# Where the last head's sample projection and the far key scores stand in one step of a hybrid decoder

## The chip, the cores and the metric

The kernel runs on one core of one Trainium2 chip. The metric is the device time of one launch in microseconds. A core has TensorE (PE), VectorE (DVE), ScalarE (ACT), GpSimd (POOL), and SyncE (SP), which here only issues DMAs. Each engine works through its own instructions in order; semaphores tie the engines together.

## The reference

One layer, for a prompt of 512 tokens and for 8 sample sequences of 4 new tokens each, which share all weights. Of the mixer, what matters here is the attention of the sample tokens to a cache of 512 keys, at three dilations:

```python
z_q, z_k, z_v, z_conv, z_mq, z_gate = split_combined(h @ lw['w_in'])
q, k, v = attention_qkv(z_q, z_k, z_v, pos, lw)           # per-head RMSNorm and partial rotary
k_all = jnp.concatenate([cache_k, k], axis=1)             # 8 x (512 + 4) x 4 heads x 128
for g, (window, dilation) in enumerate(((128,1), (512,4), (2048,16))):
    o, l = dilated_gather_attention(q[:, :, 4*g:4*g+4], k_all, v_all, window, dilation)
a = combine_dilated(outs, lses) @ lw['w_attn_proj']
c = conformer_tail(conv of glu(z_conv)); m = memory attention(z_mq) @ lw['w_mem_proj']
x1 = x + (sigmoid(g_a)*a + sigmoid(g_c)*c + sigmoid(g_m)*m) @ w_out
y  = x1 + hier_moe(rms_norm(x1))                          # 32 experts, 6 MB of weights each
state: k_win_sample = k_all[:, 4:], v_win_sample = v_all[:, 4:], ...
```

## The kernel before

**Stages.** The program first normalises and transposes the inputs, then takes four heads in turn, then the conformer input (the "glu" products), the attention of the sample tokens, three gated output branches, `w_out` and the routing, and at last 32 experts whose 201 MB of weights stream in from HBM.

**A head.** `project_head(h, units)` multiplies the transposed tokens with three 128x8x256 weight units (queries of two dilations; queries of the third and keys; values and memory queries). Each unit is split into a high and a low part, the high by ACT and the low by DVE (`split`, line 231), and each product takes three matmuls (lines 237 to 239). `norm_vecs` (line 377) then norms the heads: squares on ACT, the root on POOL, the scaling on DVE. `attend_head(h)` computes the prompt's attention of a head: scores into PSUM, exponentials, transposes, copies of them by DVE (`PT`, lines 507 and 541), products with the values. The list scheduler lets the attention of head h run among the products of head h+1. The PSUM pool `mm`, through which all products go, has three buffers, so a product waits until the norms of the one three before it have been read out.

**The sample part of a head.** `sample()` inside `project_head` computes the 32 sample tokens' heads from the unsplit units (48 matmuls, line 404). It writes two queries per head to DRAM scratch, `q1d` and `q2d`, by DMAs that POOL issues (lines 415 and 416).

**Far scores.** Dilations 4 and 16 over the cache are done on DVE and not as matmuls. `far_scores(b)`, for each of the 8 sequences, loads 1 MB of cached keys and 1 MB of the queries, which are broadcast from `q1d` to all 128 partitions, multiplies them (line 591) and sums (line 592). `wide_scores(a)` does the same twice for the other dilation from `q2d` (lines 601 and 602). All of them are written ahead of the last head's attention (`h == 3`). `q1d` holds all four heads, so the first broadcast load waits for the sample part of the last head.

**Buffers and the load queue.** Units, cached keys, broadcasts and values all lie in `ring`, six buffers of 1 MB. SP issues nearly all loads, in one order that the scheduler fixes. A load whose buffer is still read holds up every load behind it.

**After the heads.** `glu(c)` multiplies conformer unit c with the tokens (lines 694 to 696). Three units follow the heads; the fourth (`c3`) is multiplied in the sample section. There `mem_scores(bp)` and `weighted(...)` compute the scores against the cached memory keys and the weighted sums of cached values (line 918). Then `branch_loads` fetches and splits the first weights of the output branches, and `branch` starts. The 16 new cache rows (`k_win_sample`, `v_win_sample`) are written by POOL (lines 688 and 690).

Of the kernel before, what the change touches and what calls it, by code (L numbers as in the profile page):

```python
# [11 lines left out]
F32 = mybir.dt.float32  # L12
# [5 lines left out]
ALU = mybir.AluOpType  # L18
# [3 lines left out]
P = 128  # L22
# [4 lines left out]
DB = 8  # L27
# [125 lines left out]
def build(tc, I, O, cols):  # L153
# [44 lines left out]
    def nm(s):  # L198
        cnt[0] += 1
        return f"{s}_{cnt[0]}"  # L200
# [4 lines left out]
    def v8(t):  # L205
        return t.rearrange("p (k c) -> p k c", k=8)
# [159 lines left out]

    def norm_vecs(ps, A, vecs, gains, rows):
        n = len(vecs)
        ms = hs_.tile([P, 4], F32, name=nm("hms"), tag="hms", bufs=4)
        sq = hs_.tile([P, HD], BF16, name=nm("sq"), tag="sq")  # L370
        for q, (pv, av) in enumerate(vecs):
            nc.scalar.activation(sq[:rows], ps[pv], AF.Square, scale=SC, accum_out=ms[:rows, q:q + 1])
        r = hs_.tile([P, 4], F32, name=nm("hrs"), tag="hrs", bufs=4)
        nc.gpsimd.tensor_scalar(r[:rows, :n], ms[:rows, :n], EPS, None, op0=ALU.add)
        nc.gpsimd.tensor_tensor(r[:rows, :n], r[:rows, :n], nhalf[:rows].to_broadcast([rows, n]), op=ALU.pow)
        for q, (pv, av) in enumerate(vecs):
            nc.vector.scalar_tensor_tensor(A[av], ps[pv], r[:rows, q:q + 1], gains[q],
                                           op0=ALU.mult, op1=ALU.mult)
# [17 lines left out]
    def project_head(h, units):  # L396
# [3 lines left out]
        def sample():  # L400
            psS = mm.tile([P, 512], F32, name=nm("mm"), tag="mm")
            for k in range(8):
                for j, u in enumerate((2, 0, 1)):
                    nc.tensor.matmul(psS[32 * j:32 * j + 32, :256], hTs[:, k, :], v8(units[u])[:, k, :],
                                     start=(k == 0), stop=(k == 7))
            sA = hs_.tile([P, 2, HD], F32, name=nm("sA"), tag="sA", bufs=1)
            s3 = psS[:96, :256].rearrange("p (c d) -> p c d", c=2)
            idx = [(slice(0, 96), c, slice(0, HD)) for c in range(2)]
            norm_vecs(s3, sA, [(x, x) for x in idx], [gsm[:96, 0], gsm[:96, 1]], 96)
            nc.scalar.copy(vS[:32, h, :], psS[:32, 0:HD])  # L410
            sc_, ss_ = rope_t[:96, 2 * P:2 * P + 32], rope_t[:96, 2 * P + 32:CF0 - P]
            rope(sA[:96].unsqueeze(1), sc_.unsqueeze(1).unsqueeze(1).to_broadcast([96, 1, 2, 32]),
                 ss_.unsqueeze(1).unsqueeze(1).to_broadcast([96, 1, 2, 32]), [96, 1, 2])
            nc.gpsimd.tensor_copy(kS[64:96, h, :], sA[64:96, 1, :])
            nc.gpsimd.dma_start(q1d[:, :, h, :].rearrange("b t d -> (b t) d"), sA[32:64, 1, :])
            nc.gpsimd.dma_start(q2d[:, :, h, :].rearrange("b t d -> (b t) d"), sA[64:96, 0, :])
            psT = tr.tile([P, 512], F32, name=nm("tr"), tag="tr")
            for c in range(2):
                nc.tensor.transpose(psT[:, c * 96:(c + 1) * 96], sA[:96, c, :], ident[:96, :96])
            nc.vector.tensor_copy(Ts[:, h].rearrange("p a q -> p (a q)"), psT[:, :192])  # L420
# [50 lines left out]
    def attend_head(h, T, vh, vp):  # L471
# [48 lines left out]
        for ip in range(2):  # L520
# [20 lines left out]
            nc.vector.tensor_copy(PT, pt.rearrange("p a b t -> p (a b) t"))  # L541
# [43 lines left out]
    marks = []  # L585

    def far_scores(b):
# [3 lines left out]
        nc.vector.tensor_tensor(qb, kb, qb, op=ALU.mult)  # L591
# [3 lines left out]
    def wide_scores(a):  # L595
# [5 lines left out]
        nc.vector.tensor_tensor(qb, kb, qb, op=ALU.mult)  # L601
# [31 lines left out]
    TV = project_head(0, w0)  # L633
    for h in range(4):
        nxt = [load_cols(w_in, c) for c in cols_h(h + 1)] if h < 3 else None
        if h == 3:
            def cload(c, t=None):
                return load_cols(w_in, [(CCOL + c * P, P), (CCOL + 512 + c * P, P)], t)

            cu = []  # L640
            for c in range(NGH):
                far_scores(2 * c)
                far_scores(2 * c + 1)
                cu.append(cload(c))
            far_scores(6)
            far_scores(7)
            for a in range(2):
                wide_scores(a)
# [110 lines left out]

    for c in range(NGH):  # L760
        glu(c, cu[c], st_tile)
        glus[0] += 1
# [5 lines left out]
    trs = tr  # L768

# [160 lines left out]
    for bp in range(2):  # L930
        mem_scores(bp)
    far_rows()
# [7 lines left out]
    for bp in range(2, 4):  # L940
        mem_scores(bp)
# [8 lines left out]
    glu(3, c3, kt_tile, ring)  # L950
    glus[0] += 1
# [734 lines left out]
```

## Time and profile before

| | us |
|---|---|
| median of 3 runs | 1192.67 (1192.16 to 1195.36) |
| the profiled execution | 1193.17 |
| its span, first to last instruction | 1191.4 |
| PE busy | 1112.9 (93%) |
| DVE busy | 526.5 (44%) |
| ACT, POOL busy | 294.9, 291.4 |
| DMA read and written | 324 MB, 272 GB/s |

A share of the whole span says little here, since the stages have different limits. The rows below therefore go by stretches of the span. A busy PE counts overlapping matmuls once, and a PE at the lower clock is busy as well.

### The profile page before, as it was taken

The numbers are of one execution on the slowest core, as the hardware profiler recorded it, in microseconds if no ns is written. First come the engines' busy times: TensorE is split into PE (matmuls) and PEld (weight loads), VectorE is DVE, ScalarE is ACT, GpSimd is POOL, SyncE is SP. The second block draws the span as 40 slices with busy tenths as digits, with TensorE's granted clock in tenths as the row PEclk, the third lists the DMA queues.
The fourth block names the chain that finished last, engine by engine and source line by source line (L and its number), as shares of the span: only waits on it lengthen the run. The fifth ranks groups of instructions, "written<-read, shape, count | busy, mean of one in ns | idle before, by whom it ended". The sixth has DMA issues, their size and how long they took to land. (4 is left out here: it accounts for less than half of the span.)

```text
span 1191.4 us, 21761 instructions
## 1 busy us (share of the span) xinstructions
PE 1112.9 (93%) x8964; PEld 827.6 (69%) x8965; DVE 526.5 (44%) x974; ACT 294.9 (25%) x723; POOL 291.4 (24%) x465
## 2 busy tenths in 40 slices
PE   6999999989289999999999998999999999999986
PEld 5998888988174899999998853555555555555442
DVE  6634444596385799947433255112224211122111
ACT  7433443432032432244322223000000000000000
POOL 5453434560048520212223010111111111111111
PEclk9999999999699999999999998999999999999998
DMA  9952210497867998313309377999999999999995
GB/s 323 230 156 76 62 38 28 170 369 218 217 254 257 365 381 311 106 36 107 142 6 353 128 301 292 413 409 411 415 413 410 412 412 408 407 391 405 405 408 228
DMA packets 116036, 323.85 MB, mean 272 GB/s; under 512 B 15273, under 2 KB 72177, under 8 KB 88032
## 3 DMA queue, kind: packets, MB, share of 16 engines
q1 hardware_dynamic: 105520, 310.10, 69.2%
q0 software_dynamic: 7664, 10.70, 3.8%
q10 hardware_dynamic: 2752, 1.65, 0.5%
q8 instruction: 71, 1.16, 0.4%
q14 instruction: 29, 0.24, 0.1%
HBM read 310.18 MB, written 31.49 MB: 287 GB/s over the span
## 5 line engine op out<-in xcount | busy, mean ns | idle before, releaser
L694 PE MATMUL mm<-hTh,hi 128*128 128x272 f32 x512 | 150.8, 295 | 7.5 <-DVE u L745 6.4
L1540 POOL DMA_INDIRECT out_y_all<-work,ids x32 | 49.9, 1558 | 437.5 <-DVE work L1539 399.7
L696 PE MATMUL mm<-hTh,lo 128*128 128x272 f32 x512 | 149.7, 294 | 0.0
L695 PE MATMUL mm<-hTl,hi 128*128 128x272 f32 x512 | 149.4, 292 | 0.0
L1536 PE MATMUL pd<-w,work 128*64 128x512 f32 x512 | 119.3, 608 | 0.6 <-issue 0.6
L1516 PE MATMUL pu<-w,xgT 128*64 128x256 f32 x992 | 113.5, 380 | 4.6 <-DMA w<-in_w_expert_up 3.5
L1516 PE MATMUL pg<-w,xgT 128*64 128x256 f32 x992 | 112.9, 380 | 1.2 <-DVE xgT L1336 0.9
L237 PE MATMUL mm<-hi,hTh 128*128 128x256 f32 x384 | 110.3, 287 | 0.0
L239 PE MATMUL mm<-hi,hTl 128*128 128x256 f32 x384 | 110.1, 287 | 0.0
L238 PE MATMUL mm<-lo,hTh 128*128 128x256 f32 x384 | 110.0, 286 | 0.0
L1516 PEld LDWEIGHTS pg<-w,xgT 128*64 128x64 f32 x992 | 71.0, 137 | 49.8 <-issue 16.2
L1526 DVE TENSOR_TENSOR work<-work,pu 128x256 f32<-128x256 f32 x32 | 19.5, 608 | 194.5 <-PE pu L1516 194.5
L694 PEld LDWEIGHTS mm<-hTh,hi 128*128 128x128 f32 x512 | 98.2, 192 | 10.3 <-DVE u L745 6.9
L1516 PEld LDWEIGHTS pu<-w,xgT 128*64 128x64 f32 x992 | 70.5, 137 | 43.0 <-DMA w<-in_w_expert_up 6.6
L695 PEld LDWEIGHTS mm<-hTl,hi 128*128 128x128 f32 x512 | 98.3, 192 | 0.5 <-issue 0.4
L696 PEld LDWEIGHTS mm<-hTh,lo 128*128 128x128 f32 x512 | 97.9, 192 | 0.4 <-issue 0.4
L231 DVE TENSOR_TENSOR lo<-w,hi 128x2048 fp32r<-128x2048 f32 (+2 forms) x46 | 82.1, 1802 | 35.9 <-ACT hi L230 35.9
L715 DVE SCALAR_TENSOR_TENSOR cT<-u,cT 128x512 f32<-128x512 f32 x120 | 88.9, 763 | 1.3
L1536 PEld LDWEIGHTS pd<-w,work 128*64 128x64 f32 x512 | 34.6, 139 | 62.8 <-issue 59.8
L1330 PE MATMUL px<-h,ohs 64*64 64x512 f16 (+1 forms) x558 | 72.4, 388 | 4.8 <-DVE gates L1412 2.9
L1026 POOL TENSOR_TENSOR z<-z,gth 128x272 f32<-128x272 f32 x32 | 35.6, 1116 | 163.9 <-DVE gth L1025 163.9
L237 PEld LDWEIGHTS mm<-hi,hTh 128*128 128x128 f32 x384 | 72.5, 189 | 2.3 <-issue 2.2
(459 smaller groups left out, 2058.8 us busy)
## 6 DMA issues: line engine op xcount, KB each, us to landing
w<-in_w_expert_gate SPq DMA_DIRECT2D x64, 1024.0 KB, 10.5
w<-in_w_expert_up SPq DMA_DIRECT2D x64, 1024.0 KB, 10.4
w<-in_w_expert_down SPq DMA_DIRECT2D x64, 1024.0 KB, 10.5
w<-in_w_in SPq DMA_DIRECT2D x30, 512.0 KB, 7.0
w<-in_w_in SPq DMA_DIRECT2D x12, 1024.0 KB, 13.0
w<-in_cache_k SPq DMA_DIRECT2D x10, 1024.0 KB, 11.4
w<-q1d SPq DMA_DIRECT2D x8, 1024.0 KB, 11.3
out_k_win_sample<-in_cache_k SPq DMA_DIRECT2D x8, 1016.0 KB, 14.5
```

The lines of the kernel that those rows point to most:

```text
L231: last_lo[0] = e.tensor_tensor(lo[:, s], v8(t)[:, s], hi[:, s].bitcast(F32), op=ALU.subtract)
L237: nc.tensor.matmul(ps, xh[k], wh[k], start=(k == 0), stop=False)
L238: nc.tensor.matmul(ps, xh[k], wl[k], start=False, stop=False)
L239: nc.tensor.matmul(ps, xl[k], wh[k], start=False, stop=(k == n - 1))
L694: nc.tensor.matmul(ps, wh[k], xh[k], start=(k == 0), stop=False)
L695: nc.tensor.matmul(ps, wh[k], xl[k], start=False, stop=False)
L696: nc.tensor.matmul(ps, wl[k], xh[k], start=False, stop=(k == n - 1))
L715: nc.vector.scalar_tensor_tensor(cTf[:, c, :NP], u[:, c, j:j + NP], w, cTf[:, c, :NP], op0=ALU.mult, op1=ALU.add)
L1330: nc.tensor.matmul(px[CAP * f:CAP * f + CAP], oh[:64 if i == 4 else P, i, :], src[:, 4 * f:4 * f + 4, :], start=(i == GORD[0] and r == 0), ...
L1516: last = nc.tensor.matmul(ps[CAP * f:CAP * f + CAP], xT[:, k, :], ws[k // 4][:, k % 4, 256 * f:256 * f + 256], start=(k == 0), stop=(k == 7))
L1536: last = nc.tensor.matmul(pd[CAP * f:CAP * f + CAP], hT[:, kk % 2, CAP * (kk // 2):CAP * (kk // 2) + CAP], w[4 + kk // 2][:, kk % 2, 512 * ...
L1540: nc.gpsimd.indirect_dma_start(out=y2, out_offset=bass.IndirectOffsetOnAxis(ap=idc2, axis=0), in_=o, in_offset=None, bounds_check=2 * NT - ...
```

## The change

- `sample` becomes a function of its own. For the last head it is called inside the projection of the third head (index 2), at its second unit and with high priority. To have the weights there, the units of heads 2 and 3 are loaded together, after head 0.
- `q1d` and `q2d` are written by SP and not by POOL.
- The far scores of sequences 0 to 2 are written ahead of the third head's attention, those of 3 to 7 ahead of the last head's. Each product is done in two halves of 1024 columns, and is held behind the last norm of the third head's projection (`far_pin`).
- The two wide scores come after the heads, and their products are held behind the last copy of attention probabilities (`last_att`).
- The fourth conformer unit is multiplied before the weighted sums, right after all memory scores, and the values of sequences 4 and 5 are loaded after it.
- The new cache rows are written by SP, after the load of that unit.

```diff
-    def project_head(h, units):
+    def sample(h, units):
 ...
-            nc.gpsimd.dma_start(q1d[:, :, h, :].rearrange("b t d -> (b t) d"), sA[32:64, 1, :])
-            nc.gpsimd.dma_start(q2d[:, :, h, :].rearrange("b t d -> (b t) d"), sA[64:96, 0, :])
+        nc.sync.dma_start(q1d[:, :, h, :].rearrange("b t d -> (b t) d"), sA[32:64, 1, :])
+        nc.sync.dma_start(q2d[:, :, h, :].rearrange("b t d -> (b t) d"), sA[64:96, 0, :])
 ...
+    def project_head(h, units, nxt=None):
 ...
                 if u * 2 + ip == (SPOS if h == 0 else 0):
-                    sample()
+                    if h < 3:
+                        sample(h, units)
+                if nxt is not None and (u, ip) == (1, 0):
+                    with tc.high_priority():
+                        sample(h + 1, nxt)
 ...
-        nc.vector.tensor_tensor(qb, kb, qb, op=ALU.mult)
+        for f in range(2):
+            fs = slice(1024 * f, 1024 * f + 1024)
+            with tc.issue_after(far_pin[0].ins):
+                nc.vector.tensor_tensor(qb[:, fs], kb[:, fs], qb[:, fs], op=ALU.mult)
 ...
-        nc.vector.tensor_tensor(qb, kb, qb, op=ALU.mult)
+        with tc.issue_after(last_att[0].ins):
+            nc.vector.tensor_tensor(qb, kb, qb, op=ALU.mult)
 ...
     for h in range(4):
-        nxt = [load_cols(w_in, c) for c in cols_h(h + 1)] if h < 3 else None
+        for g in {0: (1,), 1: (2, 3)}.get(h, ()):
+            U[g] = [load_cols(w_in, c) for c in cols_h(g)]
+        if h == 2:
+            far_pin.append(last_norm[0])
+            for b in range(3):
+                far_scores(b)
 ...
             for c in range(NGH):
-                far_scores(2 * c)
-                far_scores(2 * c + 1)
                 cu.append(cload(c))
+                far_scores(3 + c)
             far_scores(6)
             far_scores(7)
-            for a in range(2):
-                wide_scores(a)
 ...
-            TV = project_head(h + 1, nxt)
-    for b in range(DB):
-        nc.gpsimd.dma_start(O["k_win_sample"][0, b, PAST - DT:], kS[64 + DT * b:64 + DT * b + DT])
-    for b in range(DB):
-        nc.gpsimd.dma_start(O["v_win_sample"][0, b, PAST - DT:], vS[0 + DT * b:0 + DT * b + DT])
+            TV = project_head(h + 1, U[h + 1], U[3] if h == 1 else None)
 ...
+    for a in range(2):
+        wide_scores(a)
     for c in range(NGH):
         glu(c, cu[c], st_tile)
 ...
-    vs = [v_load(b) for b in range(4)]
-    vs += [v_load(4, "hi"), v_load(5, "lo")]
     mks += [pair_load(mk_src, 2), pair_load(mk_src, 3)]
     c3 = cload(3, wslot("hi"))
+    new_rows()
+    vs = [v_load(b) for b in range(4)]
 ...
-    for bp in range(2):
+    for bp in range(4):
         mem_scores(bp)
+    glu(3, c3, kt_tile, ring)
+    glus[0] += 1
+    vs += [v_load(4, "hi"), v_load(5, "lo")]
     far_rows()
```

Of DVE's order before, the end of the last head's projection: `w` are ring buffers (keys and queries of the far scores), `lo` is a low part of a unit, `A` the normed heads of the product that the PSUM buffer of the first glu product held before.

```order
L591 TENSOR_TENSOR w_3260<-w_3259,w_3260 128x2048
L541 COPY PT_2716<-tr_2711 128x512
L592 TENSOR_REDUCE S_100<-w_3260 128x4x4
L591 TENSOR_TENSOR w_3266<-w_3265,w_3266 128x2048
L541 COPY PT_2740<-tr_2735 128x512
L592 TENSOR_REDUCE S_100<-w_3266 128x4x4
L420 COPY Ts<-tr_2797 128x192
L231 TENSOR_TENSOR lo_3684<-w_3271,hi_3683 128x2048
L377 SCALAR_TENSOR_TENSOR A_3080<-mm_3031,hrs_3087,gq 128x128
L377 SCALAR_TENSOR_TENSOR A_3080<-mm_3031,hrs_3087,gk 128x128
```

The same place on DVE after the change, ending at the norms of the same product.

```order
L600 TENSOR_TENSOR w_3296<-w_3295,w_3296 128x1024 x2
L535 TENSOR_SCALAR m_2794<-m_2794 128x2
L541 TENSOR_SCALAR P_2772<-P_2772,den_2771 128x256 x2
L601 TENSOR_REDUCE S_100<-w_3296 128x4x4
L513 COPY PT_2753<-tr_2749 128x256
L539 RECIPROCAL den_2795<-den_2795 128x2
L600 TENSOR_TENSOR w_3303<-w_3302,w_3303 128x1024 x2
L541 TENSOR_SCALAR P_2796<-P_2796,den_2795 128x256 x2
L601 TENSOR_REDUCE S_100<-w_3303 128x4x4
L547 COPY PT_2785<-tr_2780 128x512
L547 COPY PT_2809<-tr_2804 128x512
L379 SCALAR_TENSOR_TENSOR A_3101<-mm_3052,hrs_3108,gq 128x128
```

Before, four far scores stand ahead of these norms and four behind them; now all eight stand ahead, and the last of them directly so.

DVE before, in the last head's attention: the two wide scores (`S_101`) among the copies `PT` that PE waits for.

```order
L507 COPY PT_3384<-tr_3381 128x128
L601 TENSOR_TENSOR w_3302<-w_3301,w_3302 128x2048
L499 TENSOR_TENSOR P_3435<-P_3435 128x96
L500 RECIPROCAL m_3434<-m_3434 128x1
L745 SCALAR_TENSOR_TENSOR u<-st_3737,mm_3687 128x272
L602 TENSOR_REDUCE S_101<-w_3302 128x4x4
L601 TENSOR_TENSOR w_3314<-w_3313,w_3314 128x2048
L528 TENSOR_REDUCE m_3511<-S_3508 128x2
L507 COPY PT_3420<-tr_3416 128x256
```

DVE after, at the end of the last head's attention.

```order
L547 COPY PT_3510<-tr_3505 128x512
L759 SCALAR_TENSOR_TENSOR u<-st_3893,mm_3843 128x240
L761 SCALAR_TENSOR_TENSOR us<-st_3893,mm_3843 128x8x4
L547 COPY PT_3534<-tr_3529 128x512
L611 TENSOR_TENSOR w_3541<-w_3540,w_3541 128x2048
L611 TENSOR_TENSOR w_3553<-w_3552,w_3553 128x2048
L612 TENSOR_REDUCE S_101<-w_3541 128x4x4
L612 TENSOR_REDUCE S_101<-w_3553 128x4x4
```

No attention copy stands behind a wide score any more; all four wide instructions follow the last copy.

SP before, at the end of the sample section: values, memory values, and the first weights of the branches.

```order
L846 DMA w_4374<-in_cache_v 128x2048
L846 DMA w_4376<-in_cache_v 128x2048
L852 DMA w_4420<-in_cache_mem_v 128x2x512 x2
L852 DMA w_4423<-in_cache_mem_v 128x2x512 x2
L852 DMA w_4426<-in_cache_mem_v 128x2x512 x2
L852 DMA ws_4417<-in_cache_mem_v 128x2x512 x2
L218 DMA w_4600<-in_w_in 128x8x256
```

SP after, the same place.

```order
L863 DMA w_4507<-in_cache_v 128x2048
L869 DMA ws_4550<-in_cache_mem_v 128x2x512 x2
L863 DMA w_4509<-in_cache_v 128x2048
L869 DMA w_4553<-in_cache_mem_v 128x2x512 x2
L869 DMA w_4556<-in_cache_mem_v 128x2x512 x2
L869 DMA w_4559<-in_cache_mem_v 128x2x512 x2
L218 DMA w_4608<-in_w_in 128x8x256
```

The loads are nearly the same, but `w_4553`, `w_4556`, `w_4559` and `w_4608` now lie in the ring buffers of the values of sequences 0 to 3, which the first weighted sum reads to its end; and the fourth conformer unit's matmuls stand ahead of that sum on PE.

## Rows read from the trace of the kernel before

**Rows 1.** Busy time by stretches of the span; header line says the columns.
```profile
core 0: us, PE busy (x) PEld busy (x) DVE busy (x) ACT busy (x) POOL busy (x), PEclk, DMA share, GB/s
205.20:260.00 54.80, 51.69 (x448) 46.48 (x442) 38.99 (x64) 23.90 (x85) 32.14 (x53) 1.00 0.68 242
260.00:297.90 37.90, 36.21 (x310) 31.80 (x310) 27.82 (x42) 7.98 (x19) 6.62 (x16) 1.00 0.81 245
297.90:325.70 27.80, 4.22 (x17) 3.90 (x17) 8.40 (x9) 0.08 (x1) 0.00 (x0) 0.62 0.87 210
325.70:350.80 25.10, 21.53 (x180) 19.68 (x181) 22.87 (x42) 5.94 (x20) 8.22 (x19) 0.88 0.71 272
350.80:401.20 50.40, 48.81 (x446) 30.57 (x444) 29.59 (x63) 17.47 (x34) 43.22 (x99) 1.00 0.81 285
401.20:680.00 278.80, 278.80 (x2237) 269.77 (x2239) 170.01 (x265) 95.04 (x173) 57.77 (x87) 1.00 0.52 187
740.00:1160.00 420.00, 404.72 (x3085) 212.28 (x3085) 93.67 (x191) 28.47 (x59) 46.75 (x30) 1.00 1.02 409
```
**Rows 2.** PE in order of time: start us, us, instruction, [idle before <- releaser].
```profile
260.04 0.39 PE L694 MATMUL mm<-hTh,hi 128*128 128x272 f32 x1 [0.96 <-DVE A L377]
...
303.64 0.59 PE L694 MATMUL mm<-hTh,hi 128*128 128x272 f32 x1 [5.75 <-DVE u L745]
...
325.73 0.56 PE L511 MATMUL tr<-vh,PT 128*128 128x128 f32 x1 [17.87 <-DVE PT L507]
...
346.90 1.10 PE L544 MATMUL tr<-PT,mv 128*128 128x256 f32 x4 [2.24 <-DVE PT L541]
...
349.73 1.10 PE L544 MATMUL tr<-PT,mv 128*128 128x256 f32 x4 [1.29 <-DVE PT L541]
...
401.11 0.39 PE L694 MATMUL mm<-hTh,hi 128*128 128x272 f32 x1
```
**Rows 3.** DVE in order of time.
```profile
204.64 0.61 DVE L377 SCALAR_TENSOR_TENSOR A<-mm,hrs,gmq 128x128 f32<-128x128 f32 x2 [0.26 <-POOL hrs L375]
...
228.37 2.40 DVE L591 TENSOR_TENSOR w<-w,w 128x2048 f32<-128x2048 f32 x1 [0.97 <-DMA w<-q1d]
...
300.72 2.29 DVE L601 TENSOR_TENSOR w<-w,w 128x2048 f32<-128x2048 f32 x1 [9.50 <-DMA w<-q2d]
...
322.36 2.29 DVE L601 TENSOR_TENSOR w<-w,w 128x2048 f32<-128x2048 f32 x1 [16.58 <-DMA w<-in_cache_v]
```
**Rows 4.** Waits of the load queue: us in total, times, longest.
```profile
SPq L590 <- DMA q1d<-sA: 73.5, 1, 73.5
```
**Rows 5.** Busy time, as in rows 1, of two stretches at the lower clock.
```profile
303.60:307.90 4.30, 4.22 (x17) 3.90 (x17) 2.19 (x1) 0.00 (x0) 0.00 (x0) 0.50 1.07 200
...
325.70:331.80 6.10, 6.07 (x31) 5.49 (x32) 6.07 (x13) 0.94 (x3) 0.00 (x0) 0.50 0.98 370
```
**Rows 6.** Groups of instructions: xcount | busy us, mean ns | idle before.
```profile
L404 PE MATMUL mm<-w,hTs 128*32 128x256 f32 x192 | 16.8, 383 | 0.0
...
L591 DVE TENSOR_TENSOR w<-w,w 128x2048 f32<-128x2048 f32 x8 | 18.4, 2305 | 1.6 <-DMA w<-q1d 1.5
L592 DVE TENSOR_REDUCE S<-w 128x16 f32<-128x2048 f32 x8 | 18.3, 2282 | 0.1
...
L231 DVE TENSOR_TENSOR lo<-w,hi 128x1024 fp32r<-128x1024 f32 x6 | 7.2, 1222 | 5.2 <-ACT hi L230 5.2
```
**Rows 7.** DMA issues: xcount, KB each, median us from issue to landing.
```profile
w<-q1d SPq DMA_DIRECT2D x8, 1024.0 KB, 11.3
...
w<-q1d SPq DMA_DIRECT2D x1, 1024.0 KB, 4.3
...
w<-in_w_in SPq DMA_DIRECT2D x1, 1024.0 KB, 10.0
```
**Rows 8.** SP and ACT in order of time, end of the sample section.
```profile
371.83 4.45 SPq L852 DMA_DIRECT2D w<-in_cache_mem_v  x6
...
383.64 0.42 SPq L218 DMA_DIRECT2D w<-in_w_in  x1
...
394.04 1.90 ACT L230 CAST hi<-w 128x2048 fp32r<-128x2048 f32 x1
```

More of the change, by code (lines that the diff above doesn't have):

```diff
@@ L365, in cols_h @@
                 ((VCOL + h * P, P), (MQCOL + h * P, P)))
+    last_norm, far_pin = [None], []
     def norm_vecs(ps, A, vecs, gains, rows):
@@ L376, in norm_vecs @@
         for q, (pv, av) in enumerate(vecs):
-            nc.vector.scalar_tensor_tensor(A[av], ps[pv], r[:rows, q:q + 1], gains[q],
-                                           op0=ALU.mult, op1=ALU.mult)
+            last_norm[0] = nc.vector.scalar_tensor_tensor(A[av], ps[pv], r[:rows, q:q + 1], gains[q],
+                                                          op0=ALU.mult, op1=ALU.mult)
     def rope(A4, c4, s4, shape):
@@ L394, in bc4 @@
         return w.unsqueeze(2).to_broadcast([P, 2, 2, 32])
-    def project_head(h, units):
+    def sample(h, units):
+        psS = mm.tile([P, 512], F32, name=nm("mm"), tag="mm")
+        for k in range(8):
+            for j, u in enumerate((2, 0, 1)):
+                nc.tensor.matmul(psS[32 * j:32 * j + 32, :256], hTs[:, k, :], v8(units[u])[:, k, :],
+                                 start=(k == 0), stop=(k == 7))
+        sA = hs_.tile([P, 2, HD], F32, name=nm("sA"), tag="sA", bufs=2)
+        s3 = psS[:96, :256].rearrange("p (c d) -> p c d", c=2)
+        idx = [(slice(0, 96), c, slice(0, HD)) for c in range(2)]
+        norm_vecs(s3, sA, [(x, x) for x in idx], [gsm[:96, 0], gsm[:96, 1]], 96)
+        nc.scalar.copy(vS[:32, h, :], psS[:32, 0:HD])
+        sc_, ss_ = rope_t[:96, 2 * P:2 * P + 32], rope_t[:96, 2 * P + 32:CF0 - P]
+        rope(sA[:96].unsqueeze(1), sc_.unsqueeze(1).unsqueeze(1).to_broadcast([96, 1, 2, 32]),
+             ss_.unsqueeze(1).unsqueeze(1).to_broadcast([96, 1, 2, 32]), [96, 1, 2])
+        nc.gpsimd.tensor_copy(kS[64:96, h, :], sA[64:96, 1, :])
+        nc.sync.dma_start(q1d[:, :, h, :].rearrange("b t d -> (b t) d"), sA[32:64, 1, :])
+        nc.sync.dma_start(q2d[:, :, h, :].rearrange("b t d -> (b t) d"), sA[64:96, 0, :])
+        psT = tr.tile([P, 512], F32, name=nm("tr"), tag="tr")
+        for c in range(2):
+            nc.tensor.transpose(psT[:, c * 96:(c + 1) * 96], sA[:96, c, :], ident[:96, :96])
+        nc.vector.tensor_copy(Ts[:, h].rearrange("p a q -> p (a q)"), psT[:, :192])
+    def project_head(h, units, nxt=None):
         T = t_tile(nm("T")).bitcast(F32).rearrange("p (s t) -> p s t", s=5)
@@ L399, in project_head @@
         vp = hd.tile([P, 4, HD], F32, name=nm("vp"), tag="vp")
[L400 to L414, printed above, removed]
-            nc.gpsimd.dma_start(q1d[:, :, h, :].rearrange("b t d -> (b t) d"), sA[32:64, 1, :])
-            nc.gpsimd.dma_start(q2d[:, :, h, :].rearrange("b t d -> (b t) d"), sA[64:96, 0, :])
[L417 to L420, printed above, removed]
         for u in range(3):
@@ L540, in attend_head @@
             PT = hd.tile([P, 4, P], F32, name=nm("PT"), tag="PT")
-            nc.vector.tensor_copy(PT, pt.rearrange("p a b t -> p (a b) t"))
+            last_att[0] = nc.vector.tensor_copy(PT, pt.rearrange("p a b t -> p (a b) t"))
             po = tr.tile([P, 256], F32, name=nm("tr"), tag="tr")
@@ L583, in window_copy @@
         chained(O["v_win_sample"][0, b, 0:PAST - DT], I["cache_v"][0, b, DT:])
-    marks = []
+    marks, last_att = [], [None]
     def far_scores(b):
@@ L633, in build @@
     TV = project_head(0, w0)
+    U = {}
     for h in range(4):
-        nxt = [load_cols(w_in, c) for c in cols_h(h + 1)] if h < 3 else None
+        for g in {0: (1,), 1: (2, 3)}.get(h, ()):
[4 more added lines that the diff above has]
+                far_scores(b)
         if h == 3:
@@ L768, in build, with new_rows @@
     trs = tr
+    def new_rows():
+        for b in range(DB):
+            chained(O["k_win_sample"][0, b, PAST - DT:], kS[64 + DT * b:64 + DT * b + DT])
+        for b in range(DB):
+            chained(O["v_win_sample"][0, b, PAST - DT:], vS[0 + DT * b:0 + DT * b + DT])
     def softmax_parts(parts, outs):
@@ L939, in build @@
     weighted(PTa, 4, PTn, vs[0:4], sst("sa"), 0, aT)
-    for bp in range(2, 4):
-        mem_scores(bp)
     sample_taps(0, 3, sm)
@@ L949, in build @@
     mvt = [t[:, b2] for t in mvs for b2 in range(2)]
-    glu(3, c3, kt_tile, ring)
-    glus[0] += 1
     taps(TG[2], glu_end[0])
```

## The prediction

> **What bounds the kernel now.** I read the stretches of the span first [rows 1]. From 740 us on, the experts run at a DMA share of 1.02 and 409 GB/s: this stage takes as long as its 201 MB take, and starts when the mixer lets it. From 401.2 to 680 us PE is busy for all 278.8 us at the full clock, so the branches and `w_out` are PE's. What can be won lies ahead of 401 us. There the rows show a hole: from 297.9 to 325.7 us PE works for 4.22 of 27.8 us. PE in order of time [rows 2] gives its two halves, 5.75 and 17.87 us, and names DVE both times. But DVE itself sat still then: its order of time [rows 3] shows 9.50 us ahead of the first wide product, until its queries from `q2d` had landed, and 16.58 us ahead of the second. (That row names a load of values, which that instruction does not read; by its operands it is the second half of the `q2d` loads.) The attention copy that PE wants stands behind this product in DVE's order. So the hole is a late transfer at the head of DVE's line. Why late: the load queue's waits [rows 4] show 73.5 us, once, until the last head's query was in `q1d`. All 18 MB of the far and wide scores start after it, at 224 us.
>
> Since everything after 401.2 us follows PE's progress, I take a microsecond won there as one won at the end.
>
> **The change, part by part.** Four places, in time.
>
> *The sample projection, one head earlier.* The last head's quarter of 16.8 us [rows 6], about 4.1 us of PE, moves from behind the third head's projection into it. PE was full there, so nothing is won or lost, but the third head's last norm, at 204.64 us [rows 3], ends 4.1 us later: at about 205.2 + 4.1 = 209.3. By then `q1d` is long written, so far scores can start at 209.3 and not at 228.37 [rows 3].
>
> *When the first glu product can start.* It starts at 260.04 us, released by a DVE norm [rows 2]. That norm stands behind four far scores before, behind eight now (first pair of order rows). DVE was busy for 38.99 us between 205.2 and 260 [rows 1], of which 4 x (2.305 + 2.282) = 18.3 are far scores [rows 6]; the rest stays. A half product is 1024 wide; the nearest row is a difference of that width, 1.222 us [rows 6]. Eight far scores now take 8 x (2 x 1.222 + 2.282) = 37.8. So DVE needs 38.99 - 18.3 + 37.8 = 58.5 us, and is through at 209.3 + 58.5 = 267.8 if it never waits for data. It will wait a little. Six ring buffers carry the pairs and three conformer units, each of which keeps its buffer until its split. Following the buffers by the order, the pairs from the fifth on are asked for only 6 to 9 us before DVE is ready for them. A broadcast lands 4.3 us after its issue on an idle queue, and 11.3 us (median) on a full one [rows 7]. With loads asked for every 3 us or so, I take 8 to 9 us. That is 3 to 4 us of waiting in all, where 4.3 would give none and 11.3 some 12. So the first glu product starts at about 272 us, between 266 and 281: **12 us later than now.** The third head's attention, whose copies now stand among eight far scores, ends inside this time.
>
> *From there to the end of the heads' attention.* Now 90.8 us, 260.0 to 350.8. What goes: the hole, 5.75 + 17.87 us [rows 2], since no copy stands behind a wide product any more; half of 4.3 + 6.1 us at the lower clock, 5.2 us [rows 5]; and most of the 2.24 + 1.29 us that PE waited for the memory attention's copies, which now have transposes to stand beside them: 2.5 us. What comes: PE is short of work before 272 us, so the first 4 us run at half the clock again, as they did after 303.6 [rows 5], which costs 2.1 us. The wide scores, 9.1 us of DVE, come right after the last attention copy; PE has about 7 us of transposes and scores to do until it needs DVE, so 2 us show. Sum: -23.6 - 5.2 - 2.5 + 2.1 + 2 = **-27.2 us.**
>
> *The end of the sample section.* Today the fourth unit's matmuls run until 396.5 us beside the loads for what follows: the memory values and the first branch weights are asked for at 371.83 and 383.64, these land 10.0 us later [rows 7], ACT casts from 394.04 [rows 8], and the branch starts at 401.11 [rows 2], 4.6 us after those matmuls. Now the matmuls come first, and the weights' buffer is that of a value tile (third pair of order rows). It comes free about 8 us after the fourth unit's matmuls: the copies of the probabilities, then 16 + 8 matmuls, which took 364.6 to 370.9 before. Six half-megabyte issues take 4.45 us ahead of it [rows 8], landing 10.0, the cast 1.9, the difference 2.3, less the overlap of the last two with matmuls that need the high part alone: 24.5 us. PE has 16 us of weighted sums to do in it. So it waits 8.4 us where it had 1.6 us of idle time in the stretch (50.4 less 48.81) [rows 1]; with a clock that may fall meanwhile, **+8 us.** Bounds: nothing, if the memory values land as fast as on an idle queue, and +13 if the window copies behind them crowd the queue.
>
> *The rest.* 24 small DMAs fewer on POOL (8 of query rows, 16 of cache rows) win nothing, as POOL is not waited for there, 32.14 of 54.8 us busy [rows 1]. SP issues them instead; at 0.42 us for one issue [rows 8], the 16 cache rows take some 7 us of SP ahead of the values, which are needed 20 us later. The convolution taps, 94 us of DVE, are done in the same places as before.
>
> Sum: +12 - 27.2 + 8 = -7.2. From the profiled execution, 1193.17, that gives 1186.0; the median of the runs stands 0.5 lower, so about 1185.5, rounded to **1186 us.**
>
> **The rivals.**
>
> *All of the hole is won.* Loads land well under 8 us, so that DVE never waits (266 to 268 us), and the branch weights arrive beside the sums (+2). 1193 + 7 - 27 + 2 = 1175; with a little more of the third head's idle time gone, 1173. For it: the first pairs are loaded long ahead, on a queue with a share of 0.68 [rows 1]. Against it: the same loads in this very stretch landed at 11.3 us.
>
> What the Trainium skill has on this speaks for it: "DMA: Bandwidth & Descriptors" (Measured) puts 1 MB from HBM to SBUF at 6.15 us, for one transfer alone. By that, as an estimate, no pair waits, the first glu product starts at 268 and the sum gives 1182; no row here shows a broadcast at that figure, they show 4.3 and 11.3.
>
> *The ring becomes the bound: slower.* Two buffers per pair and three units that sit on theirs leave two pairs in flight. If a pair takes 13 us from issue to landing, each of the last five makes DVE wait some 5 us, the first glu product starts near 290, and 30 - 27 + 8 = +11 gives 1203 us. It decides from about 7 us of waiting beyond mine. For it: 11.3 us is the median of the same loads now; DVE has nothing else to do ahead of these norms, and PE nothing without them. Against it: today's loads came in a burst of buffers freed long before, so that they queued behind each other; now each is asked for when a buffer comes free.
>
> *No change: the wait moves to the end of the sample section.* SP now also carries 24 writes. If one whose source is late stops the queue, or the 16 cache rows delay the values by 7 us and these the branch weights, the +8 becomes +15, and the sum is 1193. For it: a wait on `q1d` has stopped this queue for 73.5 us already [rows 4]. Against it: the units of the last two heads stand ahead of the late writes in SP's order.
>
> The Trainium skill has a rule against this part: "Perfetto Trace Analysis" (DMA Optimizations) would give inputs to one issuing engine and outputs to another. The row of 73.5 us agrees in so far as it shows a queue stopped by one wait; it was a load that waited there, not a write.
>
> **How the numbers follow.** A difference under 0.3% (3.6 us) can't be told from none, so faster means under 1189.1 and slower over 1196.3. The forecast 0.40 (1179 to 1191, nearly all faster), the full gain 0.25, no change 0.19, slower 0.16. Faster: 0.25 + 0.36 = 0.61; within 0.3%: 0.04 from the forecast and 0.17 from no change, 0.21; slower 0.18. The range reaches from a full gain that is 3 us better than mine, 1170, to halfway into the ring's case, 1199; beyond these lie 2 in 10.
>
> **What will show it.** Right, if PE has no idle time of 17.9 us released by a copy any more, the wide products wait for nothing, and the first glu product starts between 266 and 281 us. The far products' own idle time shows the ring: under 6 us in sum for me, over 12 for the slower rival. The first branch matmul comes 20 us or more after the fourth unit's last one, released by a cast or a split of its weights; if it follows within 18, the full gain is nearer. I am wrong if the experts' stretch changes its rate, or the branches' stretch shows idle time: then a microsecond at 401 is not one at the end.

## The result

The changed kernel took 1188.33 us (median of 6 runs, 1186.77 to 1190.34) against 1195.76 for the kernel before on the same occasion: a ratio of 0.9944, 95% interval 0.9925 to 0.9963. Timed a second time, on another occasion (experiment e9), it took 1190.14 against 1193.16: 0.9976, interval 0.9965 to 0.9986. So it is faster, by something between 3 and 7 us. The traces agree with the smaller figure: the spans are 1191.4 before, 1188.3 and 1188.0 after, and the profiled executions 1193.17 and 1190.34. What follows accounts for these 3.1 us of span. That the first timing gives twice as much lies mostly with the kernel before: three of its six runs there took 1196.15 to 1197.04 us, longer than any of its 50 runs beside the experiments (1191.90 to 1195.83). What made these three longer stays open.

Four places in time divide the span. Each is read from PE in order of time; the last column is where the router's first product for the prompt tokens starts.

| us | first glu product | attention ends | first branch matmul | router |
|---|---|---|---|---|
| before | 260.04 | 350.83 | 401.11 | 648.21 |
| after | 273.16 | 336.30 | 394.87 | 645.32 |
| length of the piece, after less before | +13.1 | -27.7 | +8.3 | +3.3 |

From the router to the end both take 543 us, and the experts run at the same 1.02 and 409 GB/s as in [rows 1].

Busy time by stretches after the change, the stretches of [rows 1] (PE, PEld, DVE, ACT, POOL, granted clock, DMA share, GB/s), and the end of the sample section, 336.3 to 394.9, whose counterpart before is 350.8 to 401.1:

```profile
205.20:260.00 54.80, 49.13 (x425) 43.41 (x424) 52.17 (x70) 21.28 (x76) 24.87 (x31) 0.93 0.91 315
260.00:297.90 37.90, 30.30 (x212) 24.56 (x211) 14.33 (x40) 5.32 (x17) 5.47 (x11) 0.74 0.63 148
297.90:325.70 27.80, 27.80 (x239) 26.20 (x237) 9.96 (x27) 9.82 (x27) 1.56 (x2) 1.00 0.33 115
...
401.20:680.00 278.80, 276.19 (x2201) 266.75 (x2200) 170.52 (x258) 92.76 (x166) 91.10 (x137) 0.99 0.52 187
740.00:1160.00 420.00, 404.88 (x3084) 211.65 (x3082) 93.45 (x190) 28.51 (x59) 44.95 (x29) 1.00 1.02 409
...
336.30:394.90 58.60, 55.55 (x469) 33.42 (x467) 47.95 (x95) 18.18 (x36) 23.99 (x55) 0.97 0.82 308
```

The third row is the hole of [rows 1 to 3]: PE worked 4.22 of its 27.8 us before and works all of it now. The price shows in the second row: PE is busy for 30.30 of 37.9 us, at a granted clock of 0.74 (part of it at 1.2 GHz, part at 2.4), where it had 36.21 at 1.00. The fourth row says that the branches are no longer PE's alone: 2.6 us of idle time in a stretch that had none, and POOL is busy for 91.10 us where it had 57.77.

PE in order of time after the change (start, us, instruction, idle time before and what ended it):

```profile
250.81 0.33 PE L524 MATMUL tr<-ident,PT 128*128 128x128 f32 x1 [1.81 <-ACT PT L522]
...
253.80 1.22 PE L517 MATMUL tr<-vh,PT 128*128 128x128 f32 x4 [0.74 <-DVE PT L513]
...
265.09 2.04 PE L550 MATMUL tr<-PT,mv 128*128 128x256 f32 x4 [2.21 <-DVE PT L547]
268.93 2.04 PE L550 MATMUL tr<-PT,mv 128*128 128x256 f32 x4 [0.94 <-DVE PT L547]
...
273.16 0.37 PE L703 MATMUL mm<-hTh,hi 128*128 128x272 f32 x1
...
291.06 0.61 PE L676 MATMUL tr<-ident,st 34*128 34x34 f32 x4 [3.95 <-DMA st<-in_conv_ln_b]
...
394.87 0.40 PE L703 MATMUL mm<-hTh,hi 128*128 128x272 f32 x1 [0.40 <-ACT hi L230]
...
408.44 0.52 PE L703 MATMUL mm<-sh,ph 128*128 128x272 f32 x2 [2.52 <-ACT ph L1007]
```

And DVE:

```profile
209.32 4.62 DVE L600 TENSOR_TENSOR w<-w,w 128x1024 f32<-128x1024 f32 x4
...
259.26 2.36 DVE L600 TENSOR_TENSOR w<-w,w 128x1024 f32<-128x1024 f32 x2
...
262.06 2.28 DVE L601 TENSOR_REDUCE S<-w 128x16 f32<-128x2048 f32 x1
264.26 0.68 DVE L547 COPY PT<-tr 128x512 f32<-128x512 f32 x1
268.09 0.69 DVE L547 COPY PT<-tr 128x512 f32<-128x512 f32 x1 [3.15 <-PE tr L545]
271.93 0.35 DVE L379 SCALAR_TENSOR_TENSOR A<-mm,hrs,gq 128x128 f32<-128x128 f32 x1 [3.15 <-PE tr L453]
...
405.72 2.45 DVE L231 TENSOR_TENSOR lo<-w,hi 128x2048 fp32r<-128x2048 f32 x1 [8.41 <-ACT hi L230]
408.10 0.91 DVE L998 TENSOR_TENSOR lo<-aT,sh 128x544 fp32r<-128x544 f32 x1
```

Far products start at 209.32, and none of the eight has idle time before it: their loads were always there. But the copies `PT` of the third head's attention are issued between them. PE waits for a copy that stands behind a far score, its transposes come late, and then DVE waits twice 3.15 us for PE. The norms that the first glu product waits for are last in this exchange.

Waiting is only half of these 13.1 us. Up to the first glu product PE does the same number of matmuls in both kernels, but for a record (first row before, second after; the third is a part of the second):

```profile
0.00:260.04 260.04, 245.35 (x2183) 219.60 (x2183) 138.32 (x266) 119.51 (x383) 122.14 (x207) 1.00 0.52 156
...
0.00:273.16 273.16, 252.09 (x2182) 223.38 (x2183) 156.28 (x282) 118.97 (x383) 109.41 (x184) 0.96 0.59 179
...
250.00:273.10 23.10, 14.79 (x64) 10.15 (x65) 16.55 (x25) 7.21 (x25) 2.80 (x4) 0.56 0.66 200
```

PE is idle for 6.4 us more, and busy for 6.7 us more: while it waits again and again from 250 us on, its granted clock falls to 0.56 (1.2 GHz for most of this stretch), and the same four products `tr<-PT,mv` that take 1.03 to 1.10 us at the full clock take 2.04.

Now the end of the section. At 405.72 DVE stands at the split of the second branch weights, whose cast waited for their load until 403.78; the low part of `aT`, which needs neither, is behind it.

### The profile page after: what moved, and what is told of

Its sections match the earlier page's. It is cut to its first block, busy times and chain, and to the rows that moved or that the text cites. A ratio compares the mean times of both kernels' runs of the same rounds, so it can differ in the third digit from the quotient of the medians.

```text
span 1188.3 us, 21765 instructions
## 1 busy us (share of the span) xinstructions
PE 1123.1 (95%) x8965; PEld 831.9 (70%) x8965; DVE 527.4 (44%) x982; ACT 294.6 (25%) x723; POOL 294.3 (25%) x441
## 4 chain that ended last, share of the span: by engine, by line
PE 48%; DMA 16%; issue 9%; DVE 4%; ACT 2%; SPq 0%; POOL 0%; POOLq 0%; ACTq 0%; DVEq 0%
DMA out_y_all<-work,ids 14%; PE mm L705 7%; PE mm L704 7%; PE mm L703 7%; PE pd L1552 4%; PE pg L1532 4%; PE pu L1532 4%; PE px L1346 2%; PE mm L238 1%; PE mm L239 1%; DMA w<-in_w_in 1%; PE mm L237 1%; DVE h L1386 1%; PE mm L1398 1%; PE pl L1213 1%
## 5 line engine op out<-in xcount | busy, mean ns | idle before, releaser
L230 ACT CAST hi<-w 128x2048 fp32r<-128x2048 f32 (+2 forms) x50 | 68.0, 1389 | 26.0 <-PE mm L704 16.3
```

Source lines behind the costliest of these rows:

```text
L230: nc.scalar.copy(hi[:, s], v8(t)[:, s])
```

## The experiments

Each set of four ran on one chip with the kernel before; ratios are to that. The same kernel's ratio differs by 0.3% between two occasions, as above, so across sets I compare spans and traces. A span in the table is that of the one profiled execution. The runs of one kernel on one chip have spans up to 4.8 us apart (e11: 1180.8 to 1185.6), so a difference of 2 or 3 us between two of them is not shown by the spans alone.

| | median us | ratio (95%) | span us | first glu | attention ends | branch | router |
|---|---|---|---|---|---|---|---|
| e1 end undone | 1188.05 | 0.9950 (0.9937 to 0.9964) | 1188.8 | 274.01 | 336.88 | 398.17 | 645.32 |
| e2 two far later | 1184.13 | 0.9915 (0.9902 to 0.9929) | 1182.4 | 271.01 | 329.62 | 385.89 | 638.69 |
| e3 whole products | 1192.30 | 0.9985 (0.9976 to 0.9994) | 1191.4 | 273.46 | 334.89 | 391.92 | 647.96 |
| e4 wide back | 1210.50 | 1.0139 (1.0123 to 1.0154) | 1208.6 | 305.33 | 363.21 | 419.75 | 665.33 |
| e5 wide alone | 1188.03 | 0.9962 (0.9948 to 0.9976) | 1186.1 | 259.95 | 334.40 | 391.78 | 642.93 |
| e6 copies later | 1191.21 | 0.9984 (0.9975 to 0.9993) | 1189.0 | 273.52 | 336.98 | 395.46 | 646.02 |
| e7 e2 and e6 | 1186.46 | 0.9946 (0.9933 to 0.9960) | 1183.7 | 271.20 | 330.05 | 386.17 | 640.25 |
| e8 writes on POOL | 1200.15 | 1.0063 (1.0049 to 1.0076) | 1197.9 | 280.37 | 343.61 | 400.64 | 654.93 |
| e9 changed kernel | 1190.14 | 0.9976 (0.9965 to 0.9986) | 1188.0 | 273.19 | 336.16 | 394.73 | 644.84 |
| e10 taps first | 1188.49 | 0.9968 (0.9957 to 0.9979) | 1185.6 | 273.47 | 334.51 | 396.96 | 642.82 |
| e11 e2 and e10 | 1184.61 | 0.9933 (0.9919 to 0.9947) | 1180.8 | 269.40 | 328.04 | 392.16 | 638.03 |
| e12 four far later | 1193.15 | 1.0001 (0.9992 to 1.0010) | 1190.8 | 268.71 | 340.33 | 401.54 | 647.38 |

(The branch of e5 starts with six matmuls at 391.78 us and goes on at 396.56.)

### Which part closes the hole: e4 and e5

```diff
-        with tc.issue_after(last_att[0].ins):
-            nc.vector.tensor_tensor(qb, kb, qb, op=ALU.mult)
+        nc.vector.tensor_tensor(qb, kb, qb, op=ALU.mult)
 ...
             far_scores(7)
+            for a in range(2):
+                wide_scores(a)
 ...
-    for a in range(2):
-        wide_scores(a)
```

> The two wide scores are written ahead of the last head's attention again, and their products are not held behind its last copy; nothing else. By the order they then stand on DVE ahead of the norms that the first glu product waits for. Theory (what kept PE idle was a wide product at the head of DVE's line whose queries had not landed; the early sample projection alone does not cure it): DVE waits there until the second query load lands, near 283 to 286 us, the first glu product starts near 288 to 291, 14 us later, and DVE's 9.1 us behind the last copy go: 1196 to 1202 us. Rival (the cure was the early sample projection, which takes the load queue's 73.5 us wait away, and the place of the wide scores is free): 1186 to 1190 us.

DVE of e4, then PE:

```profile
277.38 2.29 DVE L610 TENSOR_TENSOR w<-w,w 128x2048 f32<-128x2048 f32 x1 [11.46 <-DMA w<-q2d]
...
299.63 2.29 DVE L610 TENSOR_TENSOR w<-w,w 128x2048 f32<-128x2048 f32 x1 [17.04 <-DMA w<-q2d]
...
282.74 2.04 PE L550 MATMUL tr<-PT,mv 128*128 128x256 f32 x4 [13.77 <-DVE PT L547]
...
305.33 0.59 PE L704 MATMUL mm<-hTh,hi 128*128 128x272 f32 x1 [17.82 <-DVE A L379]
```

The theory holds and was too mild: the whole hole is back, further ahead in the program, and PE waits 13.77 and 17.82 us for a copy and a norm behind these products. The second queries landed at 299.6, not at 283 to 286, so it costs 20 us of span. The early sample projection does not cure the wait: with it and the wide scores at their old place, these come earlier in DVE's order, where more stands behind them. The other way round, e5 is the kernel before with the wide scores alone moved:

> The kernel before with one part of the change alone: the two wide scores are written after the heads, and their products are held behind the last attention copy. The sample projection, the far scores and the end of the sample section stay as before. Theory (the 27.8 us hole is PE waiting for copies behind a wide product, and nothing else in the change is needed to close it): first glu product still at 260 us, no idle time of 5.7 and 17.9 us, attention ends at 320 to 327 us instead of 350.8, 10 us ahead of the changed kernel; the wide scores are done near 332 us, when the second query load has landed; some of it is given back at the branch as late loads; 1176 to 1184 us. Rival (the early projection was needed, since all 18 MB still start at 224 us: the far products of the last four sequences, or the scores behind the late wide ones, now wait for their loads): 1187 to 1194 us.

The first glu product is at 259.95 again and the two idle times are gone: one part of the change, two edits, gives 5.3 us of span, where the whole change gives 3.1. The ratio, 0.9962, lies between the two of the changed kernel, 0.9944 and 0.9976. It did not reach my 1176 to 1184, since the wait came back elsewhere. PE of e5:

```profile
323.72 1.51 PE L830 MATMUL tr<-ident,w 128*128 128x128 f32 x6 [9.52 <-DMA w<-in_cache_k]
...
353.81 0.37 PE L937 MATMUL tr<-ident,PB 128*32 128x128 f32 x1 [6.45 <-DVE PB L898]
```

The transposes of the near keys stand in PE's order ahead of the rest of the attention, and their load goes out only at 304.84 us, behind the loads of the wide scores, which wait for ring buffers. So the rival was right on what limits here: with loads that start at 224 us something has to wait for them. The early projection and far scores together remove this wait, and cost the 13 us at the first glu product; neither was run without the other.

### Where the 13 us come from: e2, e3 and e12

```diff
-            with tc.issue_after(far_pin[0].ins):
+            with tc.issue_after((pin or far_pin[0]).ins):
 ...
-            far_scores(6)
-            far_scores(7)
+            far_scores(6, last_norm[0])
+            far_scores(7, last_norm[0])
```

> The products of the last two far scores are held behind the last norm of the last head's projection, so that they stand behind the norms that the first glu product waits for. Theory (that product starts at 273 us because the third head's attention copies and these norms queue behind far scores on DVE): 9.3 us of DVE less ahead of the norms, first glu product at 264 to 268 us, nothing lost later since DVE has about 18 of 28 us free there; 1180 to 1184 us. Rival (they only move into the last head's attention, whose copies and conformer products then wait for DVE): first glu product earlier by as much, given back by 350 us, 1187 to 1190 us.

5.9 us of span less than the changed kernel, 1184.13 us: the theory in size, but not by its path. The first glu product is only 2.1 us earlier: PE waits 3.1 us less ahead of it, but its granted clock is 0.50 from 258 to 271 us here too. Most of the rest of the 6.7 us that the end of the attention gains is at the convolution rows, for which PE waits 0.9 us in two places and not 3.95. Then part is lost again behind the branch (below).

> Far products whole (2048 columns) instead of in two halves; nothing else. Theory (halves let no copy in between: in the trace both halves run one behind the other every time): no difference, 1187 to 1190 us, first glu product within 2 us of 273. Rival (the halves shorten what a copy waits for by 1.2 us, five or six times in the third head's attention): 3 to 6 us slower, 1191 to 1195 us.

```diff
-        for f in range(2):
-            fs = slice(1024 * f, 1024 * f + 1024)
-            with tc.issue_after(far_pin[0].ins):
-                nc.vector.tensor_tensor(qb[:, fs], kb[:, fs], qb[:, fs], op=ALU.mult)
+        with tc.issue_after(far_pin[0].ins):
+            nc.vector.tensor_tensor(qb, kb, qb, op=ALU.mult)
```

By the time, the rival; by the trace, not its reason. Whole products end the attention 1.4 us earlier than halves and start the branch 3.0 us earlier. From there to the router 5.6 us more are lost than in the changed kernel: PE idles 1.64 us at 412.52 for a low part of `aT` behind a DVE tap that waited 4.32 us for POOL, and its granted clock is 0.70 from 415 to 425 us, where it is 1.00 in the changed kernel.

> As the one before, with the last four far products, not two, held behind the last head's norms. Theory (in the third head's attention PE still waits some 4 us in all for copies that stand behind far scores on DVE; but four far scores, 18.6 us, no longer fit beside the last head's products, where DVE has some 18 of 28 us free): 0 to 2 us faster than with two, 1177 to 1180 us. Rival (the last head's attention copies queue behind them): 3 us slower than with two or more, 1182 to 1186 us.

Neither. It is slower by 10 us of span than e11 (8.5 us by the medians), and PE's longest wait there is not for a copy:

```profile
329.30 1.97 PE L846 MATMUL tr<-ident,w 128*128 128x128 f32 x8 [9.64 <-DMA w<-in_cache_k]
```

Far scores that stay longer hold ring buffers longer: SP asked for the near keys at 309.28 us, in e11 at 288.51. It is e5's wait.

### The end of the sample section: e1, e6, e7, e10 and e11

> Only the end of the sample section is put back as it was before the change: all values loaded ahead of the last memory keys, two memory scores behind the first weighted sum, the fourth conformer unit multiplied last. The rest of the change stays. Theory (the late branch weights cost what the traces show, 8 us by the first branch matmul and 3 us more in its first 15 us): 8 to 11 us faster than the changed kernel, 1177 to 1180 us, and the first branch matmul under 6 us behind the fourth unit's last one. Rival (the old order only worked with ring buffers that came free at 325 us; now they come free at 338 to 343, behind the wide scores, so values and memory keys are late and PE waits for these): 1186 to 1191 us.

```diff
-    for bp in range(4):
+    for bp in range(2):
         mem_scores(bp)
-    glu(3, c3, kt_tile, ring)
 ...
+    for bp in range(2, 4):
+        mem_scores(bp)
     sample_taps(0, 3, sm)
 ...
+    glu(3, c3, kt_tile, ring)
     taps(TG[2], glu_end[0])
```

No gain by the trace: 645.32 us at the router, to the digit the changed kernel's; the median, 1188.05, lies by the changed kernel's 1188.33 and 1190.14. The branch follows the fourth unit's last matmul (393.73) by 4.4 us and loses nothing later, as the theory said, but PE waits for memory keys first, and the granted clock is 0.89 over 336.9 to 398.2 us:

```profile
352.48 1.11 PE L892 MATMUL mm<-ident,w 128*128 128x128 f32 x4 [3.54 <-DMA w<-in_cache_mem_k]
355.40 0.37 PE L954 MATMUL tr<-ident,PB 128*32 128x128 f32 x1 [1.80 <-DVE PB L915]
```

The rival's mechanism, and by size a tie, so that no run shows the late branch weights as the cause of the 8.3 us: with attention over at 336 us, 14 us earlier, the loads of this section are late in either order. Next, the 3.3 us behind the branch. The window copies, which share the queue there, were moved from the first branch's hook to the second's (`window_copy(j)` from `attn_hook` to `hook`):

> The changed kernel with the 16 window copies (1 MB each) issued from the second output branch and not from the first; nothing else. Theory (in the changed kernel the second branch weights land 16 us after their issue, because window copies share the queue at a DMA share of 1.04, and PE loses 3.3 us there): that loss goes, the stretch from the first branch matmul to the router takes 247 us, not 250.5; 1184 to 1186 us. Rival (the first weights and the memory values are late because their ring buffers come free late; the copies only fill free time): no difference, 1187 to 1190 us.

> Both at once: the last two far products behind the last head's norms, and the window copies from the second branch. Theory (the two gains are at different places): 4 us from the first, and up to 5.7 us from the second, since with the earlier start the branch lost 5.7 us; 1178 to 1181 us. Rival (one stage limits both, the transfers of 340 to 430 us): no faster than the better of the two alone, 1183 to 1185 us.

Both theories fall. In e6 the second weights are cast at 399.18 and not at 403.78, 4.6 us earlier, and the branch loses as much as before; in e7 PE waits longer still. DVE of e6, and PE of e7:

```profile
412.53 0.75 DVE L724 SCALAR_TENSOR_TENSOR cT<-u,cT 128x512 f32<-128x512 f32 x1 [5.70 <-POOL cT L737]
```

```profile
408.04 0.59 PE L704 MATMUL mm<-lo,ph 128*128 128x272 f32 x1 [6.46 <-DVE lo L998]
```

Behind the weights stood POOL. The change moved its convolution taps of the sample tokens, unseen: they are written behind the fourth unit in the program, and so behind the DVE taps that this unit brings. POOL after the change:

```profile
339.87 1.14 POOL L832 COPY qall<-Ts 128x16 f32<-128x16 f32 x8
372.79 0.80 POOL L733 TENSOR_TENSOR cT<-us,u 128x96 f32<-128x96 f32 x1 [31.79 <-DVE cT L724]
```

Before, these taps ran from 345.8 us. They write the sample columns of `cT` and DVE's taps the prompt columns, and yet one waits for the other. A DVE tap then waits for POOL's last, and the low parts of `aT` stand behind it. e10 writes them ahead of the fourth unit:

```diff
+    sample_taps(0, 3, sm)
     glu(3, c3, kt_tile, ring)
 ...
-    sample_taps(0, 3, sm)
     vs += [v_load(6), v_load(7)]
```

> The changed kernel with one line moved: POOL's convolution taps of the sample tokens (93 instructions) are written ahead of the fourth conformer unit again, where they stood relative to it before the change. Theory (the change put them behind that unit, so that POOL stood idle for 31.8 us and started them at 372.8 and not at about 346 us; DVE's next tap then stands at the head of its line, waiting for POOL until 411.85 us; but in the changed kernel PE's 2.5 us at 406 to 408 us are first of all the second branch weights, which land at 403.8): up to 1 us, 1186.5 to 1189 us. Rival (POOL's late taps are what PE waits for): 3 us, 1184 to 1186 us.

> The same line moved, and the last two far products behind the last head's norms. Theory (with the branch starting at 386 us POOL's taps are the last to be ready: DVE sat 11.48 us for them, and PE lost 4.0 us at 401.5 to 405.5 us and the half clock behind it): 4 to 6 us below that kernel's 1184.1, 1178 to 1180 us. Rival (behind POOL's taps stand the second branch weights, as late as in the changed kernel): 0 to 2 us, 1182 to 1184 us.

Against e9 the median of e10 is 1.7 us lower (the ratios' intervals overlap), that of e11 another 3.9: 1184.61 us, 5.5 below the changed kernel on the same chip. Both miss their theory's reason. The branch now takes 246 us to the router, as it should, though the second weights are cast at 404.07 us in e10, no earlier than in the changed kernel (403.78); but in this order ACT also casts `aT` ahead of them, so POOL's taps are not shown as the only cause. And the same dependence cuts the other way (DVE, then PE of e10):

```profile
375.43 0.55 DVE L722 TENSOR_SCALAR cT<-u 128x512 f32<-128x512 f32 x1 [4.79 <-POOL cT L737]
375.90 8.69 DVE L724 SCALAR_TENSOR_TENSOR cT<-u,cT 128x512 f32<-128x512 f32 x13
384.51 0.40 DVE L944 COPY aT<-tr 128x16 f32<-128x16 f32 x4
...
384.97 0.69 PE L924 MATMUL tr<-ident,PE 128*128 128x128 f32 x2 [5.55 <-DVE aT L944]
```

DVE waits for POOL with the fourth unit's first tap, runs 13 more, and only then makes the copies that free PE's buffer: PE idles 5.55 us in e10 and 7.57 us in e11.

### Small writes: e8 and the control e9

```diff
-        nc.sync.dma_start(q1d[:, :, h, :].rearrange("b t d -> (b t) d"), sA[32:64, 1, :])
+        nc.gpsimd.dma_start(q1d[:, :, h, :].rearrange("b t d -> (b t) d"), sA[32:64, 1, :])
 ...
-            chained(O["v_win_sample"][0, b, PAST - DT:], vS[0 + DT * b:0 + DT * b + DT])
+            nc.gpsimd.dma_start(O["v_win_sample"][0, b, PAST - DT:], vS[0 + DT * b:0 + DT * b + DT])
```

(and the same for `q2d` and the key rows)

> The 16 new cache rows and the query rows are written by POOL again; nothing else. Theory (these DMAs cost nothing on either engine, as the prediction has it): 1187 to 1190 us. Rival (on SP the cache rows stand ahead of the values and take 12 us of its time, from 332.7 to 347 us): values and all that follows are asked for earlier, the branch starts 3 to 6 us earlier; 1182 to 1186 us.

Neither: 9.6 us of span slower. POOL of e8:

```profile
182.34 1.16 POOL L785 DMA_DIRECT2D out_v_win_sample<-vS  x2
...
183.78 3.03 POOL L785 DMA_DIRECT2D out_v_win_sample<-vS  x6
...
194.60 0.61 POOL L413 DMA_DIRECT2D q1d<-sA  x1
```

POOL issues the cache rows in the middle of the last head's rope work and writes `q1d` at 194.60; SP wrote it at 183.50. The load queue waits 46.7 us in e8, the first broadcast goes out at 196.98 instead of 185.06, and the first glu product is 7.2 us later. Whether the rows or the query writes matter more was not separated.

> The changed kernel itself, unaltered, timed beside the three others of this set on one chip. Theory (its first timing, ratio 0.9944, stands): ratio 0.993 to 0.997, about 1187 to 1190 us. Rival (that ratio owed something to the chip it was taken on): 0.998 or above.

The ratio, 0.9976, lies between theory and rival. The trace repeats the first within 0.6 us at every place of the table.

## Why the prediction was right, and where it was not

Forecast: 1186 us, 7.2 below the profiled execution. Its three terms came out in size: +13.1 us (12 predicted), -27.7 (-27.2), +8.3 (8). Only the middle one did so by the mechanism that was given for it; in the other two the size is partly luck. And the sum of -7.2 agrees with the first timing (7.4 between the medians) and not with the second (3.0) or the spans (3.1).

- *The sample projection one head earlier* holds: the third head's last norm ends at 209.4, 209.3 predicted, and the first far product starts at 209.32.
- *The first glu product* starts at 273.16, inside 266 to 281, but the step's reason failed. I expected 58.5 us of DVE work and 3 to 4 us of waiting for ring buffers. The far products waited for nothing, DVE was through with them at 264.3, and the last 9 us are the exchange of copies and transposes between PE and DVE, at half the clock. The lower clock ahead of this product, worth 6.7 of the 13.1 us, is in no term; I had put it behind the product, as 2.1 us, where the granted clock is 1.00 from 273.1 us on. I had written that the third head's attention "ends inside this time"; it was what ended it. e2 shows it: two far scores fewer there, and PE has its copies sooner.
- *The hole* closed as predicted, by the place of the wide scores (e4, e5). The memory attention's waits of 2.24 and 1.29 us are gone, and the wide scores after the last copy show no idle time of PE at all, where I had 2 us. The 3.95 us at the convolution rows, and the half clock behind them (0.50 from 291 to 296 us), I had not seen; the errors nearly cancel.
- *The end of the sample section* cost +8.3; the first branch matmul came 26.0 us after the fourth unit's last, released by the cast of its weights, as written. But PE waited little: it is busy for 55.55 of 58.6 us, where it was for 48.81 of 50.4. Some 3.4 us of what came in are 24 small transposes that ran behind the start of the branch before; the rest was not followed. The 16 cache rows took SP 12.4 us, not 7; no run separates what that cost.
- *"A microsecond won there as one won at the end"* failed: the branch gave back 3.3 us. That is most of the difference between -7.2 and the -3.1 of the spans. I listed idle time in the branches' stretch as what would make me wrong, and it is there. I had also read the taps as "done in the same places as before"; DVE's start 15 us later (343.22 us, 327.96 before), POOL's 27.
- *24 small DMAs "win nothing"* failed (e8): with the early projection POOL is on the path that sets when the far loads start. The trace of before could have shown it, as the load queue's 73.5 us end with a write that POOL issues. POOL before:

```profile
213.85 2.04 POOL L690 DMA_DIRECT2D out_v_win_sample<-vS  x4
215.90 0.34 POOL L387 TENSOR_TENSOR sA<-sA,rp 96x64 f32<-96x64 f32 x1
221.18 0.23 POOL L374 TENSOR_SCALAR hrs<-hms 128x4 f32<-128x4 f32 x1 [4.94 <-ACT sq L372]
...
221.72 0.57 POOL L415 DMA_DIRECT2D q1d<-sA  x1
```

The cache rows stand in the middle of the rope work there too, and the query, done at 216.24 us, is written 5.5 us later, behind a wait for ACT.

- *"All 18 MB" after 224 us* is 19: 15 of the far scores, whose first keys are loaded earlier, and 4 of the wide.

Of the rivals, the ring did not bind. The load queue was stopped by a write, by that of the last head's query, which went out at 183.50 us:

```profile
SPq L413 <- DVE sA L379: 29.5, 2, 25.5
```

No run shows that this cost anything: the next load in the queue, the first broadcast, reads what is written, and no far product waited. The Trainium skill's suggestion in "Perfetto Trace Analysis" (DMA Optimizations), inputs by one engine and outputs by another, points the wrong way here: e8 is the nearer to it and slower by 9.6 us of span.

The best versions found are e2, with the last two far products behind the last head's norms, and e11, with the sample taps ahead of the fourth unit as well. e2 beats the kernel before by 0.0085 (interval 0.0071 to 0.0098), e11 by 0.0067 (0.0053 to 0.0081), and the changed kernel on its chip by 5.5 us. e11's profiled span is 1.6 us the shorter, but it belongs to its fastest run. The two were not timed side by side, so it is not shown that moving the taps gains anything on top of e2.

## What to carry to other kernels

A wait for a load costs what stands behind the waiting instruction on its in-order engine, so the cure is the place of that instruction, and moving its producer earlier may only bring it to a worse place. When a piece of code is moved past others, list for every engine what now comes behind what, POOL included: here untouched lines, POOL's taps and the load of the near keys, became the next limit again and again. And when several edits come together, run each alone: one of them alone gave about the time of the whole (e5), and another, which looked like housekeeping, was needed to keep it in the whole (e8).

## What the runs showed of the hardware

POOL's small tap took six times as long where DVE worked on a 128x2048 split. POOL of the changed kernel:

```profile
394.34 0.35 POOL L736 TENSOR_TENSOR stmp<-us,u 128x96 f32<-128x96 f32 x1
...
395.24 2.29 POOL L736 TENSOR_TENSOR stmp<-us,u 128x96 f32<-128x96 f32 x1
```

The split ran from 394.85 for 2.46 us, and the tap ends 0.2 us after it. The Trainium skill, "Trainium Architecture — The Big Picture" (What this means for kernel authors), has DVE and GpSimd share a port by an exclusive lock; these two rows agree. Beside DVE's 0.73 us taps POOL's took about 0.7 us.
